# A streaming-encoder trunk on one core: the order of taps and weight splits, one more plain unit, meta values in two passes, the last part by token tile

## The chip, the core and the metric

The kernel runs on one core of one Trainium2 chip. The metric is the device time of one execution in microseconds (us). The engines are named as in the profile: PE is TensorE (matmuls), PEld its weight loads, DVE is VectorE, ACT is ScalarE, POOL is GpSimd, SP is SyncE, which issues most DMAs. Each engine runs its own instructions in the order of the program; where one needs another's result, it waits for a semaphore.

## The reference, cut to what matters

```python
D_MODEL, SEQ, DEPTH, N_META = 1024, 512, 2, 16      # D_FF = 2752, CONV_WIDTH = 31, RET_HEADS = 4
def swiglu_ffn(x, w13, w2):
    a, u = jnp.split(x @ w13, 2, axis=-1)
    return (jax.nn.silu(a) * u) @ w2

def token_mix(h, w_in, ...):
    z = h @ w_in
    xp, ca, cg, q, k, v, g = jnp.split(z, splits, axis=-1)
    y_pool = pool_mixer(xp, pool_w, pool_scale)          # trailing means over 2, 4, 8, 16 tokens
    y_conv = conv_module(ca, cg, ...)                    # u = ca*sigmoid(cg); 31 taps along the tokens; LN; silu; matmul
    y_ret = retention(q, k, v, g, ret_gn_g)              # 4 heads: rotary on q and k, decayed scores, norm, silu(g)
    return jnp.concatenate([y_pool, y_conv, y_ret], axis=-1) @ w_out

def reference(x, meta, ...):
    h = jnp.concatenate([meta, x], axis=1)               # 16 + 512 tokens
    h = layer_norm(h, ln_in_g, ln_in_b)
    for l in range(DEPTH):
        h = layer_norm(ALPHA * h + 0.5 * swiglu_ffn(h, ffn1_w13[l], ffn1_w2[l]), ...)
        h = layer_norm(ALPHA * h + token_mix(h, w_in[l], ...), ...)
        h = layer_norm(ALPHA * h + 0.5 * swiglu_ffn(h, ffn2_w13[l], ffn2_w2[l]), ...)
    return h[:, N_META:]
```

## The kernel before

**Products.** All large products are done in a 32-bit format of PE with the inputs split in a rounded part and a rest (`hi`, `lo`). One product is three matmuls: hi x hi, hi x lo, lo x hi (`mm3`, lines 130 to 135). A weight tile is loaded by SP into a raw buffer, ScalarE casts it to hi, and DVE subtracts to get lo, 512 columns at a time (`weights`, lines 86 to 95). There are five hi and five lo buffers (`WB`), so the split of a weight waits until PE is done with the one five before it.

**Tokens.** Features lie on the partitions. The 528 tokens are two halves, s = 0 and 1, of 256 tokens and 8 meta tokens each: 264 columns. In the last FFN the meta tokens are left out, 256 columns.

**Stages.** They follow each other on PE: f0a, mixer m0, f0b for layer 0, then f1a, m1 and f1b (`last_ffn`) for layer 1. The hidden units of an FFN (22 pieces of 128) are done in five parts (`PARTS`; the first is units 0, 1, 21, 2, 3), and after each part its share of the second product is added to the residual h. The units 0, 1 and 21 of the first part are plain: both halves by both weight columns, 96 matmuls for a unit of two weight tiles. All other units are "summed": from sums of token halves and of weight quarters (`sums`, `sum_weights`), seven products of 12 matmuls take the place of eight. The sums of the tokens are made once in each FFN by DVE, after its norm, and are needed by the first summed unit, which is unit 2.

**Norms.** Between stages stands a layer norm (`normed`, `center`, `inv_var`, `inv_spread`): PE sums over the partitions with a matmul by ones; DVE makes the inverse root in some ten small steps that each wait for the one before (`inv_root`); PE spreads the result again. Half 0 is normed while PE still does half 1's last products. `rooted["first"]` and `rooted["second"]` are the last steps of the two roots. `tc.issue_after(x)` holds the instructions inside it behind x in the order of x's engine.

**Mixer.** First the products for the convolution (`u`) and the pool (`xp`) are made, then the values `v` in five token tiles (four of 128 and the 16 meta tokens, v4), then a loop over the heads with key, query and gate projections (`kp`, `qp`, `gp`, 24 matmuls for a half). Each goes to one of four accumulator banks (`BANKS["acc"]`). DVE turns k and q (`rotary`, the first product reads and so empties the bank), POOL copies the meta columns of k (`km`) for the scores. The convolution's 62 taps (31 for each of two tiles `m0y`) run on DVE, all of them on the same two tiles; the loop takes `PACE[hd]` of them from a generator after each projection:

```python
            for i, _ in enumerate(work(hd, before)):
                for _ in range(PACE[hd]):
                    next(taps, None)
```

**What sets the order.** A scheduler goes through the instructions in program order as a priority and puts on each engine the first one whose inputs and buffers it has. Buffers of a pool (`wide` has 16) are given out in program order. So an instruction far behind in the program can be done early if its engine is free, as the taps are.

**The end.** The last part of the last FFN goes over the two column halves; in the second the token tiles 0 to 3 follow each other, and each is normed and written (`measure`, `root`, `scale`, `leave`).

## Time and profile before

| | |
|---|---|
| median of 3 runs | 1979.4 us (1978.49 to 1981.81) |
| profiled execution | 1979.3 us, span 1977.5 us |
| busy: PE, DVE, ACT, POOL | 1912.4, 1548.9, 920.1, 215.0 us |
| instructions | 36739 |

The span is the time from the first instruction to the last one in the profile; the 1.8 us to the execution's own time lie around it. PE is the engine to look at; DVE, the next, is busy for 78% of the span.

### The profile page before, as it was taken

What the parts mean: (1) busy time and instruction counts of PE and PEld (TensorE: products, weight loads), DVE (VectorE), ACT (ScalarE), POOL (GpSimd) and SP (SyncE); (2) the same over time, 40 slices, a digit from 0 to 9 for tenths busy, and PEclk for the clock granted to TensorE, in tenths of its full rate; (3) what the DMA queues carried; (4) which work ended last, traced back from release to release, by engine and by line L of the source; (5) the groups of instructions that cost most, each with busy time, mean ns of one, the idle gap of its engine ahead of it and who ended that gap; (6) DMA issues with size and microseconds to landing.
All of it is one profiled execution on the core that took longest, in us unless ns stands there. A gap on an engine that the chain in (4) does not pass through costs nothing.

```text
span 1977.5 us, 36739 instructions
## 1 busy us (share of the span) xinstructions
PE 1912.4 (97%) x14423; PEld 1826.3 (92%) x14423; DVE 1548.9 (78%) x3466; ACT 920.1 (47%) x1845; POOL 215.0 (11%) x283
## 2 busy tenths in 40 slices
PE   7999999999999999999999999999999999999996
PEld 6999999997899899999989999998889998999995
DVE  7788778689767977788697787787897697877787
ACT  5454446443333644454464554464343265544451
POOL 4000000442003000000120000005320130000001
PEclk9999999999999999999999999999999999999998
DMA  4422323322112233323213323332131213323321
GB/s 143 129 86 97 116 88 104 100 76 85 63 34 75 64 98 108 97 89 107 95 54 111 101 89 107 97 118 75 65 104 54 65 44 118 107 86 107 107 97 43
DMA packets 61069, 177.98 MB, mean 90 GB/s; under 512 B 6976, under 2 KB 10944, under 8 KB 60896
## 3 DMA queue, kind: packets, MB, share of 16 engines
q1 hardware_dynamic: 59744, 174.59, 27.8%
q8 instruction: 113, 1.85, 0.4%
q10 hardware_dynamic: 1152, 1.05, 0.2%
q14 instruction: 60, 0.49, 0.1%
HBM read 173.52 MB, written 2.10 MB: 89 GB/s over the span
## 4 chain that ended last, share of the span: by engine, by line
PE 79%; DVE 12%; POOL 3%; issue 3%; ACT 2%; DMA 0%; SPq 0%; DVEq 0%; POOLq 0%; ACTq 0%
PE f0a_y L134 2%; PE f0a_y L133 2%; PE f1bo L890 2%; PE f1bo L888 2%; PE f0a_y L135 2%; PE f1bo L889 2%; PE f0b_y L134 2%; PE f1a_y L134 2%; PE f0b_y L133 2%; PE f0b_y L135 2%; PE f1a_y L135 2%; PE f1a_y L133 2%; DVE m0y L610 1%; DVE m1y L610 1%; PE m0sc L719 1%
## 5 line engine op out<-in xcount | busy, mean ns | idle before, releaser
L610 DVE SCALAR_TENSOR_TENSOR m1y<-m1u,vec,m1y 128x528 f32<-128x528 f32 x60 | 46.1, 801 | 0.0
L91 ACT CAST f0a_o_h<-f0a_o_r 128x512 fp32r<-128x512 f32 (+1 forms) x37 | 23.5, 635 | 48.4 <-PE f0a_y L134 29.5
L610 DVE SCALAR_TENSOR_TENSOR m0y<-m0u,vec,m0y 128x528 f32<-128x528 f32 x60 | 45.9, 801 | 0.0
L91 ACT CAST f1a_o_h<-f1a_o_r 128x512 fp32r<-128x512 f32 (+1 forms) x37 | 23.6, 637 | 48.0 <-PE f1a_y L134 29.0
L91 ACT CAST f0b_o_h<-f0b_o_r 128x512 fp32r<-128x512 f32 (+1 forms) x37 | 23.5, 636 | 47.6 <-PE f0b_y L134 29.3
L335 DVE TENSOR_TENSOR x<-x,f0a_y 128x264 f32<-128x264 f32 x64 | 27.1, 425 | 23.3 <-PE f0a_y L135 23.1
L335 DVE TENSOR_TENSOR h<-h,f0b_y 128x264 f32<-128x264 f32 x64 | 27.1, 425 | 23.2 <-PE f0b_y L135 23.1
L335 DVE TENSOR_TENSOR h<-h,f1a_y 128x264 f32<-128x264 f32 x64 | 27.1, 424 | 23.1 <-PE f1a_y L135 23.0
L94 DVE TENSOR_TENSOR f1bw_l<-f1bw_r,f1bw_h 128x512 fp32r<-128x512 f32 x42 | 27.7, 688 | 17.6 <-ACT f1bw_h L91 17.0
L949 POOL TENSOR_TENSOR yt<-yt,g_last 128x256 f32<-128x256 f32 x4 | 3.0, 740 | 337.2 <-ACT yt L948 337.2
L94 DVE TENSOR_TENSOR f0a_o_l<-f0a_o_r,f0a_o_h 128x512 fp32r<-128x512 f32 (+1 forms) x42 | 26.6, 642 | 13.4 <-ACT f0a_o_h L91 11.3
L94 DVE TENSOR_TENSOR f1a_o_l<-f1a_o_r,f1a_o_h 128x512 fp32r<-128x512 f32 (+1 forms) x42 | 26.7, 642 | 13.4 <-ACT f1a_o_h L91 11.4
L94 DVE TENSOR_TENSOR f0b_o_l<-f0b_o_r,f0b_o_h 128x512 fp32r<-128x512 f32 (+1 forms) x42 | 26.7, 642 | 12.6 <-ACT f0b_o_h L91 10.4
L278 POOL TENSOR_TENSOR f0b_ln_s<-h,h 128x264 f32<-128x264 f32 x2 | 1.6, 820 | 313.8 <-DVE h L335 313.8
L587 POOL MEMSET m1u<- 128x30 f32 x2 | 0.2, 123 | 307.6 <-PE f1a_20Q L135 307.6
L587 POOL MEMSET m0u<- 128x30 f32 x2 | 0.2, 123 | 306.1 <-PE f0a_20Q L135 306.1
L91 ACT CAST f1bw_h<-f1bw_r 128x1024 fp32r<-128x1024 f32 (+1 forms) x22 | 22.2, 1011 | 21.0 <-PE f1bo L890 4.2
L894 DVE TENSOR_TENSOR yt<-yt,f1bo 128x256 f32<-128x256 f32 x80 | 27.8, 414 | 5.4 <-PE f1bo L890 5.3
L291 ACT ACTIVATE m_ln_q<-h 128x264 f32<-128x264 f32 (+1 forms) x32 | 11.9, 414 | 39.7 <-DVE h L289 36.1
L257 PE MATMUL tr<-ident,xtok 128*128 128x128 f32 (+1 forms) x48 | 10.9, 328 | 12.1 <-DVE xtok L242 11.4
L281 POOL TENSOR_TENSOR m_ln_s<-m_ln_s,h 128x264 f32<-128x264 f32 (+1 forms) x20 | 18.2, 912 | 32.0 <-DVE h L329 26.1
L257 PEld LDWEIGHTS tr<-ident,xtok 128*128 128x128 f32 (+1 forms) x48 | 6.8, 167 | 16.1 <-issue 14.8
(10805 smaller groups left out, 9335.0 us busy)
## 6 DMA issues: line engine op xcount, KB each, us to landing
f1bw_r<-in_w2last SPq DMA_DIRECT2D x20, 512.0 KB, 3.8
f0a_o_r<-in_w SPq DMA_DIRECT2D x32, 256.0 KB, 2.7
f0b_o_r<-in_w SPq DMA_DIRECT2D x32, 256.0 KB, 2.8
f1a_o_r<-in_w SPq DMA_DIRECT2D x32, 256.0 KB, 2.9
m0wo_r<-in_w_out SPq DMA_DIRECT2D x8, 512.0 KB, 3.5
m1wo_r<-in_w_out SPq DMA_DIRECT2D x8, 512.0 KB, 3.5
m0w_r<-in_w_in SPq DMA_DIRECT2D x6, 512.0 KB, 4.4
m1w_r<-in_w_in SPq DMA_DIRECT2D x6, 512.0 KB, 4.3
```

The costliest lines, as they stand in the source:

```text
L91: nc.scalar.copy(out=hi[:, :n], in_=w[:, :n])
L94: e.tensor_tensor(out=lo[:, sl], in0=w[:, sl], in1=raw(hi[:, sl]), op=ALU.subtract)
L133: nc.tensor.matmul(out, lhsT=wh, rhs=xh, start=start, stop=False, skip_group_check=onto)
L134: nc.tensor.matmul(out, lhsT=wh, rhs=xl, start=False, stop=False, skip_group_check=onto)
L135: nc.tensor.matmul(out, lhsT=wl, rhs=xh, start=False, stop=stop, skip_group_check=onto)
L335: nc.vector.tensor_tensor(out=y, in0=y, in1=ps, op=ALU.add)
L610: nc.vector.scalar_tensor_tensor(out=ys[c], in0=src, scalar=wk, in1=ys[c], op0=ALU.mult, op1=ALU.add)
L719: nc.tensor.matmul(sc[:kn, :cw], lhsT=kk[ks][:, kc : kc + kn], rhs=qq[s][:, c0 : c0 + cw], start=True, stop=True)
L888: nc.tensor.matmul(o, lhsT=hh, rhs=wh, start=part > 0 and i == 0, stop=False)
L889: nc.tensor.matmul(o, lhsT=hh, rhs=wl, start=False, stop=False)
L890: nc.tensor.matmul(o, lhsT=hl, rhs=wh, start=False, stop=i == nk - 1)
L894: nc.vector.tensor_tensor(out=y[:, :256], in0=y[:, :256], in1=o, op=ALU.add)
```

## The change

Six edits are joined.

1. Taps: 28 (`EARLY`) are taken ahead of the loop over the heads; then `PACE` is (1, 1, 2, 2, 0) instead of (4, 3, 3, 2, 0), and each of these taps is held behind the last rotary sum or gate (`made["last"]`). A step of the scores comes ahead of the taps.
2. Splits: the casts and subtractions of the weights of the plain units, and of the mixer's first products, are held behind the norm's first or second root; their DMAs no longer are. `center` puts every other square in another tag's buffers.
3. Unit 2 is plain (`PLAIN = 4`), so unit 3 is the first summed one.
4. v4: hi and lo of the meta tokens lie in one stationary tile of 48 columns (hi, 16 zeros set by POOL, lo). Each weight part then needs one matmul, 16 instead of 24, and a copy and an add join the two results in a new `wide` tile, `vm`.
5. The last part of the last FFN runs over the token tiles, with both column halves of each. Tiles 0 to 2 are normed on ACT, tile 3 on DVE and ACT.
6. At the start the meta rows are scaled on ACT instead of POOL, and first.

```diff
-PACE = (4, 3, 3, 2, 0)
+EARLY, PACE = 28, (1, 1, 2, 2, 0)
@@ weights
-        nc.scalar.copy(out=hi[:, :n], in_=w[:, :n])
-        for c in range(0, n, 512):
-            sl = slice(c, min(c + 512, n))
-            e.tensor_tensor(out=lo[:, sl], in0=w[:, sl], in1=raw(hi[:, sl]), op=ALU.subtract)
+        with hold():
+            nc.scalar.copy(out=hi[:, :n], in_=w[:, :n])
+            for c in range(0, n, 512):
+                sl = slice(c, min(c + 512, n))
+                e.tensor_tensor(out=lo[:, sl], in0=w[:, sl], in1=raw(hi[:, sl]), op=ALU.subtract)
@@ hidden_part
-        plain = PARTS[part][: AHEAD if part == 0 else 0]
+        plain = PARTS[part][: PLAIN if part == 0 else 0]
...
-                late = "first" in rooted and i >= LATE_W
-                with tc.issue_after(rooted["second" if i >= LATE_B else "first"]) if late else nullcontext():
-                    w[u] = unit_weights(u, src, f"{name}_{u}")
+                late = part == 0 and "first" in rooted
+                held["by"] = rooted["second" if i >= LATE_B else "first"] if late else None
+                w[u] = unit_weights(u, src, f"{name}_{u}")
+                held["by"] = None
@@ mixer
+                held["by"] = rooted["first" if kind == "u" else "second"]
                 ws[kind, c] = [weights(w_in[i], 1024, f"{name}w{i}") for i in tiles]
+                held["by"] = None
...
+            pair = sq_pool.tile([P, 48], F32R, tag="xm", name=f"{name}xm{k}", bufs=KT)
+            nc.gpsimd.memset(raw(pair[:, NM:32]), 0.0)
...
+                if tt == 4:
+                    nc.tensor.matmul(ps[:48], lhsT=xm[k], rhs=wh, start=k == 0, stop=False)
+                    nc.tensor.matmul(ps[:48], lhsT=xm[k], rhs=wl, start=False, stop=k == KT - 1)
+                    continue
...
+            if tt == 4:
+                vm = wide(f"{name}vm")
+                nc.scalar.copy(out=vm[:n, :512], in_=ps[32 : 32 + n])
+                nc.vector.tensor_tensor(out=vm[:n, :512], in0=ps[:n], in1=vm[:n, :512], op=ALU.add)
+                ps = vm[:, :512]
...
         taps = conv_taps()
+        for _ in range(EARLY):
+            next(taps)
...
-                for _ in range(PACE[hd]):
-                    next(taps, None)
                 if hd == HEADS or i > 0:
                     next(steps, None)
+                with tc.issue_after(made["last"]):
+                    for _ in range(PACE[hd]):
+                        next(taps, None)
@@ last_ffn
+        for tt in range(4):
+            ts = slice((tt % 2) * P, (tt % 2 + 1) * P)
+            for ch in range(2):
+                for c, cw in ((0, 256), (256, 256)) if (tt, ch) == (3, 1) else ((0, 512),):
+                    o = acc(f"{name}l{tt}{ch}{c}")
+                    for i in range(nk):
...
             measure(tt)
             root(tt)
...
             scale(tt)
-            if tt != 2:
-                leave(tt)
+            leave(tt)
```

How the change moves instructions is seen at three places. First DVE at the first root of the norm between mixer 0 and f0b (`m_ln_v` to `m_ln_dg` are the root's steps, `f0b_..._l` splits of the next FFN's weights, `h` the residual). Before:

```order
1057 L94 TENSOR_TENSOR f0b_0u_l<-f0b_0u_r,f0b_0u_h 128x512
1058 L161 TENSOR_SCALAR m_ln_v<-m_ln_rs 88x3
1059 L94 TENSOR_TENSOR f0b_0u_l<-f0b_0u_r,f0b_0u_h 128x512
1060 L162 TENSOR_SCALAR m_ln_y<-m_ln_v,bits 88x3
1061 L328 SCALAR_TENSOR_TENSOR h_1_7692<-f0a_ln_x4h,m0mo_7667 128x264
1062 L167 SCALAR_TENSOR_TENSOR m_ln_g<-m_ln_y,m_ln_v 88x3
1063 L94 TENSOR_TENSOR f0b_1a_l<-f0b_1a_r,f0b_1a_h 128x512
1064 L169 SCALAR_TENSOR_TENSOR m_ln_w<-m_ln_g,m_ln_y 88x3
1065 L329 SCALAR_TENSOR_TENSOR h_1_7692<-f0a_ln_x4l,h_1_7692 128x264
```

After the change:

```order
1045 L168 TENSOR_SCALAR m_ln_v<-m_ln_rs 88x3
1046 L169 TENSOR_SCALAR m_ln_y<-m_ln_v,bits 88x3
1047 L174 SCALAR_TENSOR_TENSOR m_ln_g<-m_ln_y,m_ln_v 88x3
1048 L176 SCALAR_TENSOR_TENSOR m_ln_w<-m_ln_g,m_ln_y 88x3
1049 L177 SCALAR_TENSOR_TENSOR m_ln_y<-m_ln_w,m_ln_y 88x3
1050 L179 SCALAR_TENSOR_TENSOR m_ln_g<-m_ln_w,m_ln_g 88x3
1051 L333 SCALAR_TENSOR_TENSOR h_1_7683<-f0a_ln_x4h,m0mo_7658 128x264
1052 L176 SCALAR_TENSOR_TENSOR m_ln_w<-m_ln_g,m_ln_y 88x3
1053 L334 SCALAR_TENSOR_TENSOR h_1_7683<-f0a_ln_x4l,h_1_7683 128x264
```

The splits stand behind the root now. Second DVE from the value products to the first rotary product in mixer 0 (`m0y` are the taps, `m0vmu` the means of the value tiles, `m0k00r` the first rotary product). Before:

```order
663 L94 TENSOR_TENSOR m0wv_l<-m0wv_r,m0wv_h 128x512 x5
664 L608 TENSOR_SCALAR m0y_5486<-m0u_5126,vec 128x528
665 L645 TENSOR_TENSOR m0sm_2_5735<-m0sm_2_5735,inv_n 128x16
666 L647 SCALAR_TENSOR_TENSOR m0xp_5259<-m0sm_2_5735,inv_n,m0xp_5259 128x512
667 L646 TENSOR_TENSOR m0xp_5259<-m0sm_2_5735,m0xp_5259 128x16
668 L608 TENSOR_SCALAR m0y_5487<-m0u_5196,vec 128x528
...
679 L610 SCALAR_TENSOR_TENSOR m0y_5487<-m0u_5196,vec,m0y_5487 128x528
680 L684 TENSOR_REDUCE m0vmu_5581<-m0v_5556 128x4
681 L610 SCALAR_TENSOR_TENSOR m0y_5486<-m0u_5126,vec,m0y_5486 128x528
682 L685 TENSOR_SCALAR m0vmu_5581<-m0vmu_5581 128x4
```

After the change:

```order
657 L703 TENSOR_REDUCE m0vmu_5645<-m0v_5620 128x4
658 L704 TENSOR_SCALAR m0vmu_5645<-m0vmu_5645 128x4
659 L703 TENSOR_REDUCE m0vmu_5679<-m0v_5654 128x4
660 L704 TENSOR_SCALAR m0vmu_5679<-m0vmu_5679 128x4
661 L101 TENSOR_TENSOR m0wq_l<-m0wq_r,m0wq_h 128x512 x2
662 L101 TENSOR_TENSOR m0wk_l<-m0wk_r,m0wk_h 128x512 x2
663 L616 TENSOR_SCALAR m0y_5474<-m0u_5114,vec 128x528
664 L700 TENSOR_TENSOR m0vm<-m0v_5688,m0vm 16x512
665 L616 TENSOR_SCALAR m0y_5475<-m0u_5184,vec 128x528
...
693 L618 SCALAR_TENSOR_TENSOR m0y_5475<-m0u_5184,vec,m0y_5475 128x528
...
697 L724 TENSOR_TENSOR m0k00r<-m0kp_0_5769,cosb 128x264
```

The taps began ahead of the first value mean and stand now behind the fourth, behind the splits of wq and wk, and in a block ahead of the rotary product. Third POOL in mixer 0 after the change (`m1xm` are the tiles of mixer 1's meta tokens, `m0sm` the window sums); before, no row stood between the copies for `m0xm` and the window sums:

```order
92 L679 CAST m0xm_5518<-f0a_ln_x7l 128x8
93 L676 MEMSET m1xm_17769 128x16
...
100 L676 MEMSET m1xm_17811 128x16
101 L647 COPY m0sm_1_5751<-m0xp_5247 128x1
102 L650 TENSOR_TENSOR m0sm_1_5751<-m0xp_5247 128x542
103 L647 COPY m0sm_2_5754<-m0sm_1_5751 128x2
104 L650 TENSOR_TENSOR m0sm_2_5754<-m0sm_1_5751 64x541
```

Eight new memsets for the next mixer stand ahead of this mixer's window sums.

## Rows read from the trace of the kernel before

**Rows 1.** The page's busy time of each engine, share of the span, instructions.
```profile
PE 1912.4 (97%) x14423; PEld 1826.3 (92%) x14423; DVE 1548.9 (78%) x3466; ACT 920.1 (47%) x1845; POOL 215.0 (11%) x283
```

**Rows 2.** What PE waited for: us in total, times, longest us.
```profile
PE m0sc L719 <- POOL m0km L794: 3.4, 1, 3.4
PE f1b_2Q L133 <- ACT f1b_2x_hi L415: 3.1, 1, 3.1
PE f0b_2P L135 <- DVE f0b_2a_lo L431: 2.8, 1, 2.8
PE f1a_2P L135 <- DVE f1a_2a_lo L431: 2.5, 1, 2.5
PE f0b_ln_rs L189 <- DVE f0b_ln_q L298: 1.8, 1, 1.8
...
PE f0a_2P L135 <- DVE f0a_2a_lo L431: 1.1, 1, 1.1
```

**Rows 3.** Windows: length, busy us of PE, PEld, DVE, ACT, POOL; PEclk; DMA, GB/s.
```profile
360.00:400.00 40.00, 36.80 (x276) 35.16 (x275) 28.43 (x74) 16.77 (x34) 21.34 (x36) 0.96 0.16 55
455.00:483.00 28.00, 24.62 (x175) 23.31 (x174) 28.00 (x57) 14.01 (x27) 11.68 (x4) 0.88 0.40 128
...
640.00:680.00 40.00, 36.42 (x275) 35.15 (x275) 37.90 (x94) 25.58 (x60) 3.53 (x4) 0.96 0.12 34
...
1020.00:1060.00 40.00, 36.12 (x272) 34.81 (x271) 36.51 (x79) 25.88 (x58) 0.85 (x1) 0.96 0.21 60
...
1630.00:1660.00 30.00, 26.64 (x199) 25.93 (x199) 28.83 (x61) 19.88 (x40) 0.00 (x0) 0.89 0.30 91
```

**Rows 4.** Timeline of PE: start us, us, what [idle before <-releaser].
```profile
449.67 0.40 PE L680 MATMUL m0v<-m0wv_h,m0xm 128*16 128x512 f32 x1
...
455.21 0.28 PE L133 MATMUL m0kp<-f0a_ln_x0h,m0wk_h 128*128 128x264 f32 x1
...
458.12 0.28 PE L133 MATMUL m0kp<-f0a_ln_x0h,m0wk_h 128*128 128x264 f32 x1
...
666.40 0.59 PE L135 MATMUL f0b_2P<-m_ln_x0h,f0b_2a_lo 128*128 128x264 f32 x1 [2.81 <-DVE f0b_2a_lo L431]
```

**Rows 5.** Timeline of DVE in mixer 0: taps, and the first rotary product.
```profile
433.92 5.38 DVE L610 SCALAR_TENSOR_TENSOR m0y<-m0u,vec,m0y 128x528 f32<-128x528 f32 x5
...
446.15 4.15 DVE L610 SCALAR_TENSOR_TENSOR m0y<-m0u,vec,m0y 128x528 f32<-128x528 f32 x6
...
464.52 0.41 DVE L703 TENSOR_TENSOR m0k00r<-m0kp,cosb 128x264 f32<-128x264 f32 x1
```

**Rows 6.** Windows of line 610 alone, the taps.
```profile
430.00:455.00 25.00, 20.65 (x27) 1.00 0.06 22
```

**Rows 7.** Timeline of POOL in mixer 0: window sums, and a copy for the scores.
```profile
423.02 1.26 POOL L642 TENSOR_TENSOR m0sm<-m0xp 128x542 f32<-128x542 f32 x1 [11.98 <-ACT m0xp L597]
...
435.64 1.74 POOL L642 TENSOR_TENSOR m0sm<-m0sm 64x535 f32<-64x535 f32 x1
...
470.14 6.03 POOL L794 COPY m0km<-m0k01r 128x8 f32<-128x8 f32 x1
```

**Rows 8.** Timeline of DVE: the two roots of m_ln ahead of f0b.
```profile
619.88 0.67 DVE L94 TENSOR_TENSOR f0b_0u_l<-f0b_0u_r,f0b_0u_h 128x512 fp32r<-128x512 f32 x1
...
625.20 0.43 DVE L192 SCALAR_TENSOR_TENSOR m_ln_dg<-ident,m_ln_y 88x264 f32<-88x264 f32 x1
...
640.48 0.16 DVE L161 TENSOR_SCALAR m_ln_v<-m_ln_rs 88x3 f32<-88x3 f32 x1
...
642.70 0.43 DVE L192 SCALAR_TENSOR_TENSOR m_ln_dg<-ident,m_ln_y 88x264 f32<-88x264 f32 x1
```

**Rows 9.** Timeline of the end: the last matmul, and the last root's last step.
```profile
1959.53 0.28 PE L889 MATMUL f1bo<-f1bw_l,f1b_20x_h 128*128 128x256 f32 x1
...
1972.26 0.15 DVE L177 TENSOR_SCALAR f1brs_y<-f1brs_y 128x1 f32<-128x1 f32 x1
```

**Rows 10.** Timeline of PE at the start.
```profile
13.14 3.12 PE L257 MATMUL tr<-ident,xtok 8*128 8x8 f32 x11 [0.69 <-POOL xtok L244]
```

More of the change, by code (lines that the diff above doesn't have):

```diff
@@ L83, in col, with hold @@
         return vec[lo:hi, j : j + 1]
+    held = {"by": None}
+    def hold():
+        return tc.issue_after(held["by"]) if held["by"] is not None else nullcontext()
     def weights(src, n, name, e=nc.vector):
@@ L237, in enter @@
         for c in range(2):
-            for i, tt in enumerate(group):
+            for i, tt in reversed(list(enumerate(group))):
                 y = tok[tt][c]
@@ L289, in center @@
             nc.vector.tensor_tensor(out=y[:, :n], in0=y[:, :n], in1=mean[:, :n], op=ALU.subtract)
-            q.append(t(f"{name}_q{i}", "q"))
+            q.append(t(f"{name}_q{i}", "sm" if k > 2 and i % 2 else "q"))
             nc.scalar.activation(q[i][:, :n], y[:, :n], AF.Square)
@@ L697, in mixer @@
             nc.sync.dma_start(out=wpw[k][:, :256], in_=a["pw"][l][:, k * 256 : (k + 1) * 256])
+        made = {}
         def rotary(ps, s, n, nm):
@@ L704, in rotary @@
             nc.vector.tensor_tensor(out=r2[:, :n], in0=r2[:, :n], in1=sinb[:, s, :n], op=ALU.mult)
-            nc.vector.tensor_tensor(out=r[:, :n], in0=r[:, :n], in1=r2[:, :n], op=ALU.add)
+            made["last"] = nc.vector.tensor_tensor(out=r[:, :n], in0=r[:, :n], in1=r2[:, :n], op=ALU.add).ins
             return r
@@ L767, in gate @@
             g = t(f"{name}gs{hd}{s}", "g")
-            nc.scalar.activation(g[:, : no[s]], ps[:, : no[s]], AF.Silu)
+            made["last"] = nc.scalar.activation(g[:, : no[s]], ps[:, : no[s]], AF.Silu).ins
             gg.append(g)
@@ L871, in last_ffn @@
             nk = len(full)
+            if part == len(PARTS) - 1:
+                break
             for ch in range(2):
@@ L896, in last_ffn @@
                 steps = range(-1 if part == 0 else 0, nk)
-                if part == len(PARTS) - 1 and ch == 1:
-                    for tt in range(3):
-                        for i in steps:
-                            step(i, tt)
-                        for j in range(2):
-                            add(tt, j, ps[tt][:, j * 256 : (j + 1) * 256])
-                    for j in range(2):
-                        o = ps[3] if j == 0 else acc(f"{name}o{ch}4")
-                        for i in steps:
-                            step(i, 3, j * 256, 256, o[:, :256])
-                        add(3, j, o[:, :256])
-                else:
-                    for i in steps:
-                        for tt in range(4):
-                            step(i, tt)
-                    for tt in range(4):
-                        for j in range(2):
-                            add(tt, j, ps[tt][:, j * 256 : (j + 1) * 256])
+                for i in steps:
+                    for tt in range(4):
+                        step(i, tt)
+                for tt in range(4):
+                    for j in range(2):
+                        add(tt, j, ps[tt][:, j * 256 : (j + 1) * 256])
             done += nk
@@ L935, in scale @@
             for j, y in enumerate(yt[tt]):
[L936 removed]
+                if tt < 3:
                     break
@@ L956, in leave @@
                 (nc.sync if j % 2 else nc.scalar).dma_start(out=a["out"][tt * P : (tt + 1) * P, j * 256 : (j + 1) * 256], in_=y)
-        for tt in range(4):
+        c0 = done * 512
+        w_last = [[], []]
+        for i in range(0, nk, 2):
+            cw = min(2, nk - i) * 512
+            for ch, make in enumerate((weights, weights_wide)):
+                w = make(a["w2last"][ch, :, c0 + i * 512 : c0 + i * 512 + cw], cw, f"{name}l{ch}{i}")
+                w_last[ch] += w if ch else [at(w, slice(c, c + 512)) for c in range(0, cw, 512)]
+        for tt in range(4):
+            ts = slice((tt % 2) * P, (tt % 2 + 1) * P)
[3 more added lines that the diff above has]
+                    for i in range(nk):
+                        wh, wl = (x[:, c : c + cw] for x in w_last[ch][i])
+                        hh, hl = at(hid[full[i]][tt // 2], ts)
+                        nc.tensor.matmul(o[:, :cw], lhsT=hh, rhs=wh, start=i == 0, stop=False)
+                        nc.tensor.matmul(o[:, :cw], lhsT=hh, rhs=wl, start=False, stop=False)
+                        nc.tensor.matmul(o[:, :cw], lhsT=hl, rhs=wh, start=False, stop=i == nk - 1)
+                    for k in range(0, cw, 256):
+                        y = yt[tt][2 * ch + (c + k) // 256]
+                        nc.vector.tensor_tensor(out=y[:, :256], in0=y[:, :256], in1=o[:, k : k + 256], op=ALU.add)
             measure(tt)
             root(tt)
-            if tt == 3:
-                with tc.issue_after(met[tt]):
-                    leave(2)
             scale(tt)
-            if tt != 2:
-                leave(tt)
+            leave(tt)
     load_tokens((4, 0, 1))
```

27 lines of the change are left out of this document (12 added, 15 removed).

## The prediction

> **What bounds the kernel now.** The page's first part says it: TensorE (PE) is busy for 97% of the span [rows 1], and nearly all of that is matmuls that must be done. So a change gains only where PE stands idle, runs at the lower of its clock levels, or gets fewer matmuls; it loses where one of the three grows. I therefore read next the list of what PE waited for [rows 2]. It names short waits of a few kinds: at the start of each summed unit 2 (f0a_2, f0b_2, f1a_2, f1b_2, on a split made by VectorE or ScalarE), at each norm (a sum of squares or a root made by VectorE, DVE below), and in each mixer at the first scores (on GpSimd's copy m0km, 3.4 us). The windows of these places [rows 3] show idle time and clock together: in 455 to 483 PE is busy for 24.6 of 28 us at a mean clock of 0.88, in 640 to 680 for 36.4 of 40 at 0.96. The clock has two levels, 1.2 and 2.4 GHz, and a row shows the lower one behind a wait: after 2.81 us of waiting, the matmul at 666.40 takes 0.59 us [rows 4].
>
> Prices of a matmul are start to start [rows 4]: the 24 matmuls of the fifth value tile take from 449.67 to 455.21, 0.231 us each at 512 columns; the 24 of a projection take from 455.21 to 458.12, 0.121 us each at 264.
>
> **Plain unit 2, in four FFNs.** A plain unit has 2 products x 8 x 3 x 2 halves = 96 matmuls, a summed one 7 x 4 x 3 = 84. That adds 12 x 4 = 48 matmuls at 0.121 us, **5.8 us** lost. In return the first summed unit comes 96 matmuls (11.6 us) later, and DVE has to do only four splits more ahead of it (0.67 us for one in [rows 8]), 2.6 us. PE waited there 3.1, 2.8, 2.5 and 1.1 us [rows 2], far below the 9 us won, so these 9.5 us should go. With them go the slow stretches: 40 x 0.04 = 1.6 us in 640 to 680, 1.6 in 1020 to 1060, 30 x 0.11 = 3.3 in 1630 to 1660 [rows 3], 6.5 in all. Bounds: all 16 us go (gain 10.2), or the wait only moves to unit 3 (loss 5.8). In the new order of DVE the splits of unit 2 stand among the token sums and those of unit 3 right behind them, some 5 us ahead of the new need by these prices, so I take a **gain of 10**.
>
> **Splits behind the root.** In the first root of m_ln DVE comes from a split inside it at 619.88 to the end of its last step at 625.63, with more splits and residual adds in between; the second root, with almost nothing in between, takes from 640.48 to 643.13 [rows 8]. So a root gets some 3 us shorter. But PE has out-projection or FFN products to do while a first root runs, and the splits held back (0a and 0u, or the first mixer weights) now stand behind the root and ahead of the first product. What PE really loses at a norm is small: 1.8 us for the sum of squares in each FFN norm [rows 2], 3.2 us idle and 1.6 us of clock around the norm ahead of mixer 0 [rows 3]. Gain at least nothing (the splits are now what is late), at most some 2 to 3 us at each of five norms, 12 in all. I take **4.5**, nearer to nothing, because the held splits eat most of the root's gain.
>
> **Mixers: v4.** The fifth value tile needs 16 matmuls of 512 columns instead of 24: 8 x 0.231 = 1.85 us less in each mixer. It is part of the sum that follows.
>
> **Mixers: where the taps now stand.** This is the part that speaks against the change. Before, DVE does 27 of the 62 taps between 430 and 455 [rows 6], while PE does the value matmuls and asks nothing else of DVE. In the changed order (second piece of the order above) no tap stands there. The first tap stands behind the means of value tiles 0 to 3 and behind the splits of wq0 and wk1, and these need buffers that only v4's own first matmuls set free. The 28 EARLY taps then stand in one block, and ahead of the first rotary product (`m0k00r`), which is what empties the bank of `m0kp00`. PE has four banks for accumulators: after kp00, kp01, qp00 and qp01 the next projection, kp10, needs kp00's.
>
> On the times of before: v4 begins at 449.67, and its 16 matmuls end at 453.4. The first buffer comes free at about 450.6; a cast (1 us, put in by me) and four splits of 0.65 us bring the block's begin to about 454.2. A tap costs 0.69 us (six in 4.15) or 1.08 us while GpSimd works on the pool windows (five in 5.38) [rows 5]. In mixer 0 GpSimd's window sums also come late: eight memsets for mixer 1's `xm` stand ahead of them and wait for v4's matmuls (third piece of the order). They took from 423.0 to 437.4, some 12 us of it work [rows 7], so about 11 taps run at 1.08 and 17 at 0.69: 23.6 us. I put 1.5 us for the meta tile's add and mean and 1 for three window operations; then the rotary product begins at about 480.3 instead of 464.52 [rows 5], and kp10 at 480.6. PE's four projections end at 453.4 + 4 x 2.91 = 465.0. So PE stands for about **15 us** where nothing waited before.
>
> Not all of this is lost. Before, kp11 ended at about 472.7 and PE then waited until 476.2 for m0km (3.4 us, [rows 2]); after the new wait, kp10 and kp11 take 5.8 us and, as I put it, 1.7 more at the low clock, to 488, and m0km has been made meanwhile. The scores begin 12 us later. The slow stretch that before followed (28 x 0.12 = 3.4 us, [rows 3]) is then over, so 8.5 us stay. Behind that, 27 taps instead of 15 are left for the later heads, 12 x 0.69 = 8 us on a DVE with little room; I put 1.5 us for it. Mixer 0: **10 us lost**. In mixer 1 no memsets stand ahead of the window sums, all 28 taps run at 0.69 (19.3 us), and the loss is some 4 us smaller: **6.5**. Together **16.5**, v4's gain included. Bounds: nothing lost but v4's gain kept (+3.7), if the wait is hidden by something that I don't see; or 28 taps at 1.08 (30 us) in both mixers, 17 lost in mixer 0 and 15 in mixer 1.
>
> These two tap prices are rows and need no rule. The Trainium skill, "SBUF — State Buffer", section "Who interferes with whom", says that a DVE instruction with two SBUF inputs and a GpSimd one that reads SBUF exclude each other for a whole instruction; the trace agrees with it in both directions (1.08 against 0.69 us for a tap here, and a copy of 128x8 that took 6.03 us beside a dense DVE [rows 7]). By that rule the block and the window sums stretch each other, which is the slow rival below.
>
> **Start.** ScalarE takes the meta rows from GpSimd, for which PE waited 0.69 us [rows 10]: gain **0.7**, bounds 0 and 2.
>
> **End by token tile.** The last matmul begins at 1959.53 and the span ends at 1977.5 [rows 9]: nearly 18 us in which the tiles 1 to 3 are finished one between the other; the last root ends at 1972.4, 5.1 us before the end. Now only tile 3's second half follows the last matmul: an add and a statistic (0.8), aggregate (0.3), a dense root (2.65, as [rows 8]), the same 5.1, about 0.8 for one more GpSimd add, and 1 to 2 us of tile 2 still in DVE's queue: 11 us. Gain **6.5**, bounds 4 (tile 2 in the way) and 8. Its weights must all be split when the part begins; unit 20's own products run meanwhile, and I cost that at nothing; if they came late, 1 to 2 us.
>
> **Sum.** 0.7 + 10 + 4.5 + 6.5 - 16.5 = 5.2 us gained. The profiled execution took 1979.3 us (span 1977.5 and 1.8 around it), 0.1 below the median of 1979.4. Forecast: **1974 us**.
>
> **The rivals.**
> A, the block is hidden: PE finds work or the wait at kp10 is short. For it: DVE is idle in the value stage, so anything let through there shortens the block. Against it: the order on DVE is fixed, and kp10's bank has one releaser. Time: 1979.3 - 21.7 - 3.7 = 1954.
> B, on the other side, slower: the block runs at the slow price. If all 28 taps cost 1.08 us the mixers lose 17 + 15 = 32 and the time is 1979.3 - 21.7 + 32 = 1990; it decides once the mixers lose more than the 21.7 us of gains, 11 each, which in mixer 0 is a mean tap of 0.9 us. For it: the 1.08 of [rows 5]; against it: GpSimd has 12 us of work there, not 30.
> C, the stalls move and don't vanish: the wait of unit 2 turns up at unit 3 for half of its length, the held splits are late by what the root gains. The FFNs give 2 instead of 10, the norms 0: 1979.3 - 0.7 - 2 - 6.5 + 16.5 = 1987.
> D, gains and losses cancel: within 4 us of before, for instance norms at 0 and units at 8.
>
> **How the numbers follow.** The forecast with its own range, 1967 to 1981, has 0.50 (of which 0.35 below 1975.4, 0.11 within 0.2% and 0.04 above); A 0.20; B 0.15; C 0.06; D 0.09. A measurement of this kernel can tell about 0.2%, 4 us. Faster: 0.35 + 0.20 = 0.55. Same: 0.11 + 0.09 = 0.20. Slower: 0.04 + 0.15 + 0.06 = 0.25. The range leaves out the far end of A and of B: 1956 to 1990.
>
> **What would show it.** Right: no tap of m0y before the end of the value matmuls; PE idle 10 to 15 us ahead of kp10 in both mixers, released by DVE's m0k00r, with a slow clock behind it; no wait at f0b_2 or f0b_3; the last matmul about 11 us before the end. Wrong: taps at 430 to 455, or waits on unit 3's splits, or a last part that waits for its weights. The forecast fails most easily on the length of the wait at kp10.

## The result and the profile after

The changed kernel takes **2001.2 us** (median of 4 runs, 2000.0 to 2002.7) against 1979.0 beside it: a ratio of 1.011 [1.010, 1.012], slower by 22 us, outside the range of the forecast. Its profiled execution has a span of 1998.2 us, 20.7 more than before. The page's first part, to lay beside [rows 1]:

```profile
span 1998.2 us, 36754 instructions
PE 1913.1 (96%) x14455; PEld 1831.4 (92%) x14455; DVE 1529.3 (77%) x3431; ACT 915.3 (46%) x1832; POOL 196.6 (10%) x294
```

What PE waited for, the list that answers to [rows 2]:

```profile
PE m0kp L140 <- DVE m0k00r L724: 13.5, 1, 13.5
...
PE m1kp L140 <- DVE m1k00r L724: 10.9, 1, 10.9
PE f0a_0p L141 <- POOL x_l L273: 2.9, 2, 2.2
PE m1pu L141 <- DVE f1a_ln_x6l L325: 2.9, 1, 2.9
PE m0pu L141 <- DVE f0a_ln_x6l L325: 2.9, 1, 2.9
PE m0gp L142 <- DVE m0wg_l L101: 2.6, 1, 2.6
PE f1a_0p L141 <- DVE f0b_ln_x4l L323: 2.5, 2, 2.2
```

The waits of the units (f0a_2 to f1b_2) and the two on m0km and m1km are gone, as forecast (at unit 3, now the first summed one, 0.3 to 0.9 us are left in each FFN), and the wait at kp10 stands where it was forecast: 13.5 us in mixer 0, 10.9 in mixer 1. Four kinds of 2.5 us and more were not forecast: on `x6l` ahead of each mixer, on `x4l` in f1a, on `m0wg_l`, and on `x_l` at the start. The windows (busy us of each engine, then PE's mean clock) answer to [rows 3]:

```profile
400.00:455.00 55.00, 55.00 (x356) 49.45 (x355) 22.81 (x57) 18.85 (x45) 6.09 (x24) 1.00 0.28 92
455.00:500.00 45.00, 28.48 (x180) 26.02 (x178) 38.93 (x70) 13.13 (x28) 30.97 (x20) 0.77 0.10 33
640.00:680.00 40.00, 36.94 (x289) 35.51 (x289) 38.77 (x93) 24.70 (x60) 12.10 (x14) 1.00 0.23 67
1360.00:1410.00 50.00, 44.89 (x321) 42.94 (x321) 36.95 (x97) 23.51 (x51) 23.75 (x54) 0.90 0.16 54
```

DVE is busy for only 22.81 of the 55 us that hold the rest of the first products and most of the value stage (its matmuls begin at 430.30), and in the 45 us behind it PE for 28.48, at a mean clock of 0.77. The first product of mixer 1 lies in the fourth window: there too PE stands idle and then runs slower.

**The balance by stages.** For each stage I read the start of its first matmul on PE's timeline in both traces and took after minus before; the difference from one such landmark to the next is what that stretch lost (+) or gained (-):

| stretch | measured, us | forecast, us |
|---|---|---|
| start and the first units of the four FFNs (to unit 4's first matmul): +1.4 -2.2 -0.2 -3.6 | -4.6 | -10.7 |
| rest of f0a, f0b, f1a with its norm (to the next stage's first matmul): -2.4 -1.7 -2.1 | -6.2 | -4.5 for norms |
| first stage of the mixers (m0pu to m0v, m1pu to m1v): +4.0 +6.4 | +10.4 | in the row above |
| rest of the mixers (m0v to f0b_0p, m1v to f1b_0p): +15.6 +8.3 | +23.9 | +16.5 |
| rest of f1b | -0.2 | 0 |
| after the last matmul | -2.6 | -6.5 |
| sum | +20.7 | -5.2 |

The start and the units came out 6.1 us worse than forecast, the norms with the first stage of the mixers 8.7, the rest of the mixers 7.4, and the end 3.9. Of the mixers' 23.9 us, 5.5 (2.8 and 2.7) are lost from the first matmul of the output projection on.

### The profile page after: what moved, and what is told of

Same layout as the page of the kernel before. It is cut to its first block, busy times and chain, and to the rows that moved or that the text cites. A ratio compares the mean times of both kernels' runs of the same rounds, so it can differ in the third digit from the quotient of the medians.

```text
span 1998.2 us, 36754 instructions
## 1 busy us (share of the span) xinstructions
PE 1913.1 (96%) x14455; PEld 1831.4 (92%) x14455; DVE 1529.3 (77%) x3431; ACT 915.3 (46%) x1832; POOL 196.6 (10%) x294
## 4 chain that ended last, share of the span: by engine, by line
PE 79%; DVE 11%; ACT 2%; POOL 2%; issue 2%; DMA 0%; POOLq 0%; ACTq 0%; DVEq 0%; SPq 0%
PE f1a_y L141 2%; PE f0a_y L141 2%; PE f0b_y L141 2%; PE f1a_y L142 2%; PE f0b_y L142 2%; PE f0a_y L142 2%; PE f0b_y L140 2%; PE f1a_y L140 2%; PE f0a_y L140 2%; PE f1bo L916 1%; PE f1bo L914 1%; PE f1bo L915 1%; POOL m0sm L650 1%; DVE m1y L618 1%; PE m0o L759 1%
## 5 line engine op out<-in xcount | busy, mean ns | idle before, releaser
L101 DVE TENSOR_TENSOR f0b_o_l<-f0b_o_r,f0b_o_h 128x512 fp32r<-128x512 f32 (+1 forms) x42 | 26.6, 642 | 13.5 <-ACT f0b_o_h L98 11.4
L101 DVE TENSOR_TENSOR f1bw_l<-f1bw_r,f1bw_h 128x512 fp32r<-128x512 f32 x32 | 20.9, 688 | 9.5 <-ACT f1bw_h L98 9.1
L650 POOL TENSOR_TENSOR m0sm<-m0sm 64x541 f32<-64x541 f32 (+3 forms) x4 | 23.7, 5926 | 0.2
L98 ACT CAST f1bw_h<-f1bw_r 128x1024 fp32r<-128x1024 f32 x16 | 16.7, 1050 | 12.3 <-PE f1b_10Q L141 1.8
L920 DVE TENSOR_TENSOR yt<-yt,f1bo 128x256 f32<-128x256 f32 x64 | 21.9, 415 | 0.0
L262 PEld LDWEIGHTS tr<-ident,xtok 128*128 128x128 f32 (+1 forms) x48 | 6.9, 166 | 15.6 <-issue 15.0
```

The lines of the kernel that those rows point to most:

```text
L98: nc.scalar.copy(out=hi[:, :n], in_=w[:, :n])
L101: e.tensor_tensor(out=lo[:, sl], in0=w[:, sl], in1=raw(hi[:, sl]), op=ALU.subtract)
L650: nc.gpsimd.tensor_tensor(out=dst[b:, w_:], in0=cur[b:, w_:], in1=cur[b:, : W - w_], op=ALU.add)
L920: nc.vector.tensor_tensor(out=y[:, :256], in0=y[:, :256], in1=o, op=ALU.add)
```

## The experiments

Each ran on the chip beside the kernel before, whose medians there were 1979.5 to 1980.5 us. "After" is the changed kernel.

### 1. Is the block of taps late because of the taps' edit, or of the value tile's buffer?

The forecast read the block ahead of kp10 off the new order and counted it as the price of the taps' own edit. The rival was `vm`, the buffer of the new value tile: it is taken from the ring of 16 wide buffers (line 127), from which the taps' `m0y` and the window sums `m0sm` also come, and it is asked for ahead of them. If the ring hands out its buffers in the order in which they are asked for, then `vm`, which is needed only behind the last value matmuls, holds back in the order of issue all that is asked for behind it. GpSimd's window sums, which began at 423.02 [rows 7], begin at 456.69 in after, and `vm` is first written at 457.55. **vm_own** gives it a buffer of another ring:

```diff
-                vm = wide(f"{name}vm")
+                vm = wp.tile([P, 1024], F32, tag="raw", name=f"{name}vm", bufs=RAW)
```

> The changed kernel, with one line changed: the tile that joins the two results of the meta values (vm) comes from the pool of raw weights, not from the 'wide' pool, in which the tiles of the taps lie. Theory S (the slot): vm is given out ahead of the taps' tiles in the wide pool, so no tap can begin before the fifth value tile; with vm elsewhere the taps are back in the value stage, PE's waits of 13.5 and 10.9 us ahead of kp10 go, and the time falls from 2001 by 14 to 20 us, to 1981 to 1987. Rival E (the 28 early taps, or the hold behind the last rotary sum, make the block by themselves): both waits stay at over 8 us and the time stays within 5 us of 2001.

Measured: 1984.6 us, ratio 1.0024 [1.0013, 1.0036]; 16.6 us of the loss are gone, and the waits on m0k00r and m1k00r with them. In their place, from the list of PE's waits:

```profile
PE m1kp L140 <- ACT m1wk_h L98: 4.6, 1, 4.6
PE m0kp L140 <- ACT m0wk_h L98: 4.6, 1, 4.6
```

`vm` now holds one of the buffers that the weights of the keys need; a new wait, but a smaller one. **taps_old** does the opposite: `vm` as in after, the taps' edit undone.

```diff
-EARLY, PACE = 28, (1, 1, 2, 2, 0)
+EARLY, PACE = 0, (4, 3, 3, 2, 0)
...
-                with tc.issue_after(made["last"]):
-                    for _ in range(PACE[hd]):
-                        next(taps, None)
+                for _ in range(PACE[hd]):
+                    next(taps, None)
```

> The changed kernel with its first edit undone: no early taps, PACE (4, 3, 3, 2, 0), taps not held, as before; vm stays in the wide pool. Theory S: the first tap still stands behind the fourth value mean, but the taps come four to a projection and not in a block of 28; the waits ahead of kp10 shrink to a few us, DVE then has the taps to do among the heads and the time is 1990 to 2000. Rival E: the taps are back in the value stage and the time is 1979 to 1986.

Measured: 2001.7 us, 1.011 [1.009, 1.013]: no gain at all, and outside both expectations. The block ahead of kp10 is gone, but the wait only sits elsewhere, at the scores, where three or four taps now stand ahead of each step:

```profile
PE m0sc L740 <- DVE m0sm L751: 12.6, 3, 10.1
PE m1sc L740 <- DVE m1sm L751: 12.4, 3, 8.4
```

**before_v4_only** puts the value tile's edit, with `vm` wide, alone into the kernel before:

```diff
-            pair = sq_pool.tile([P, 2, NM], F32R, tag="xm", name=f"{name}xm{k}", bufs=KT)
+            pair = sq_pool.tile([P, 48], F32R, tag="xm", name=f"{name}xm{k}", bufs=KT)
...
+            if tt == 4:
+                vm = wide(f"{name}vm")
...
```

> The kernel before with the fourth edit alone: meta values in two passes, vm in the wide pool. Theory S: the taps stand behind the value stage by this edit alone; 12 to 22 us slower than before, though PE has 3.7 us less to do. Rival (the slot matters only with the early taps in a block): 2 to 4 us faster than before, or no change.

Measured: 1998.3 us, 1.009 [1.006, 1.012]. One of the six changes makes 18 us of loss by itself, with the same wait at the scores:

```profile
PE m0sc L739 <- DVE m0sm L750: 12.6, 3, 10.0
```

So the loss does not need the taps' edit. That the buffer makes it, and not the rest of the value tile's edit, is what vm_own and the next run show.

**vm_in_h** has `vm` in two half tiles of a ring that is free there, and the held splits undone (experiment 2), so that neither is left:

```diff
-                vm = wide(f"{name}vm")
+                vm = [t(f"{name}vm{q}", "h")[:, :256] for q in range(2)]
...
```

> vm_own_free_splits, but vm lies in two half tiles of the residual's pool (tag h, which the mixer leaves free) and not in the pool of raw weights. Theory W (vm in the raw pool held up the load of wk0): the 4.6 us that PE waited for m0wk_h and m1wk_h go, and it is 9 to 14 us faster than vm_own_free_splits, 1956 to 1962. Rival: those waits come back under another name and the time stays at 1967 to 1972.

Measured: 1956.0 us, 0.988 [0.985, 0.990], faster than before by 24.5. It differs from held_free_only (experiment 2, 1990.3 us) in the place of `vm` alone, so the wide buffer costs 34.3 us there. VectorE's timeline from ahead of the value stage on, in this kernel:

```profile
418.74 0.55 DVE L613 TENSOR_SCALAR m0y<-m0u,vec 128x528 f32<-128x528 f32 x1
...
426.44 1.32 DVE L613 TENSOR_SCALAR m0y<-m0u,vec 128x528 f32<-128x528 f32 x1
427.68 13.32 DVE L615 SCALAR_TENSOR_TENSOR m0y<-m0u,vec,m0y 128x528 f32<-128x528 f32 x13
...
460.06 0.41 DVE L724 TENSOR_TENSOR m0k00r<-m0kp,cosb 128x264 f32<-128x264 f32 x1
```

and in after:

```profile
457.82 1.32 DVE L616 TENSOR_SCALAR m0y<-m0u,vec 128x528 f32<-128x528 f32 x1
...
461.47 17.05 DVE L618 SCALAR_TENSOR_TENSOR m0y<-m0u,vec,m0y 128x528 f32<-128x528 f32 x25
479.51 0.17 DVE L653 TENSOR_TENSOR m0sm<-m0sm,inv_n 128x16 f32<-128x16 f32 x1 [0.98 <-POOL m0sm L650]
...
481.25 0.42 DVE L724 TENSOR_TENSOR m0k00r<-m0kp,cosb 128x264 f32<-128x264 f32 x1
```

With the same edit of the taps the first one starts 39 us earlier, and the block of 28 ends at 449.90, ahead of PE's first projection (455.85); 13 of them take 1.02 us each while GpSimd makes its window sums, and PE does not wait for it. The first rotary product comes 21 us earlier. GpSimd's eight memsets, which the forecast had in the way of the window sums, stand behind them here. How the ring holds the rest back is not shown: no trace names a buffer, and a ring of 17 was not run.

In after the matmul of kp10 that waited starts at the lower of the two clock levels (granted clock 0.50 from 481.70 to 485.00; 0.42 us for a matmul where 0.28 is usual):

```profile
481.72 0.59 PE L140 MATMUL m0kp<-f0a_ln_x0h,m0wk_h 128*128 128x264 f32 x1 [13.54 <-DVE m0k00r L724]
482.11 0.42 PE L141 MATMUL m0kp<-f0a_ln_x0l,m0wk_h 128*128 128x264 f32 x1
```

### 2. What do the held splits cost?

**vm_own_free_splits** is vm_own with the splits of the plain units and of the mixers' first weights issued as before; **held_free_only** is after (with `vm` wide) with the same edit:

```diff
-                late = part == 0 and "first" in rooted
-                held["by"] = rooted["second" if i >= LATE_B else "first"] if late else None
-                w[u] = unit_weights(u, src, f"{name}_{u}")
-                held["by"] = None
+                late = "first" in rooted and i >= 2
+                with tc.issue_after(rooted["second" if i >= LATE_B else "first"]) if late else nullcontext():
+                    w[u] = unit_weights(u, src, f"{name}_{u}")
...
-                held["by"] = rooted["first" if kind == "u" else "second"]
...
```

> vm_own, and the second edit undone: the casts and subtractions of the weights of the plain units and of the mixers' first products are held behind a root only where they were before. Theory H (the held splits come too late): the waits of the mixers' first products on f0a_ln_x6l and f1a_ln_x6l (2.9 us each) and of f1a_0p (2.5 us) go or shrink, and it is 5 to 12 us faster than vm_own. Rival R (the shorter roots pay for the splits): it is 3 to 8 us slower than vm_own, with waits at the norms' roots.

> The changed kernel (1998.2 us of span, 2001.2 median) with one edit undone: the splits of the first units and of the mixers' first weights are issued as before, not behind the norm's root. The value tile's buffer stays the wide one. If the held splits and the late value buffer cost independently of each other, the kernel loses the 14.3 us that the same edit gave beside the other buffer: about 1987 us, with PE's waits on x4l and x6l gone and those on m0kp and m1kp (13.5 and 10.9 us) still there. If they overlap (a later u stage hands the mixers work that would otherwise stand at kp), less is given back: 1992 to 2000 us and a longer wait at kp.

Measured: 1970.3 us, 0.995 [0.993, 0.997], and 1990.3 us, 1.005 [1.003, 1.007]. Holding the splits back costs 14.3 us beside the one buffer (more than the 5 to 12 expected) and 10.9 beside the other, where the two losses overlap in part. The forecast had a gain of 4.5. Both places take part, as the fastest kernel (experiment 3, 1951.5 us) shows with one of them held at a time, **held_units_alone** (the first of the two edits above left as in after) and **held_mixers_alone** (the second):

```diff
 held_units_alone
-                held["by"] = rooted["first" if kind == "u" else "second"]
 held_mixers_alone
-                held["by"] = rooted["second" if i >= LATE_B else "first"] if late else None
```

> The fastest kernel so far (1951.5 us, no held splits beyond those of before) with the splits of the FFNs' plain units held behind the norm's root, the mixers' weights free. Theory: the units have four products' weights in line and PE misses them only at x4l in the second layer (2.5 us), while the mixers' u stage misses them most; so this costs little: 1952 to 1956 us. Rival: the units are the cost (their first stretch gave 6 us less than the same edit without holding): 1960 to 1966 us.

> The fastest kernel so far (1951.5 us) with only the mixers' first input weights held behind the norm's root, the units' free. Theory: this is where the loss is: the first weights' third and fourth split come only behind the second half's subtractions, PE waits for x6l (2.9 us) in both mixers and runs at the low clock behind it: 1959 to 1964 us. Rival: 1951 to 1954 us, the units being the cost.

Measured: 1959.0 us, 0.988 [0.986, 0.991], and 1958.0 us, 0.988 [0.986, 0.990]: 7.6 and 6.6 us, together about the 14.3. My guess that the units cost little was wrong. PE's waits in the first:

```profile
PE f1a_0p L141 <- DVE f0b_ln_x4l L325: 2.6, 2, 2.3
PE m_ln_mean L290 <- DVE m_ln_s L288: 1.5, 2, 1.2
...
PE f1a_0p L140 <- ACT f0b_ln_x3h L319: 1.2, 1, 1.2
```

and in the second:

```profile
PE m1pu L141 <- DVE f1a_ln_x6l L327: 2.9, 1, 2.9
PE m0pu L141 <- DVE f0a_ln_x6l L327: 2.9, 1, 2.9
```

Of the units' loss 3.9 us lie between the first matmul of f1a and its first output product, where the first and the last wait of that list stand; the rest is not traced to one place. How the mixers' loss comes about shows in after on VectorE, at the norm of f0a (a row with x8 is eight instructions in line), and on PE:

```profile
382.40 1.28 DVE L101 TENSOR_TENSOR m0w_l<-m0w_r,m0w_h 128x512 fp32r<-128x512 f32 x2
...
391.23 2.79 DVE L294 TENSOR_TENSOR x<-x,f0a_ln_mean 128x264 f32<-128x264 f32 x8
...
394.35 0.97 DVE L325 SCALAR_TENSOR_TENSOR f0a_ln_x6l<-x,vec,f0a_ln_x6h 128x264 fp32r<-128x264 f32 x1
...
396.13 0.68 DVE L101 TENSOR_TENSOR m0w_l<-m0w_r,m0w_h 128x512 fp32r<-128x512 f32 x1
```

```profile
395.37 0.47 PE L141 MATMUL m0pu<-f0a_ln_x6l,m0w_h 128*128 128x264 f32 x1 [2.92 <-DVE f0a_ln_x6l L325]
395.64 0.42 PE L142 MATMUL m0pu<-f0a_ln_x6h,m0w_l 128*128 128x264 f32 x1
```

On VectorE in before, at the same norm:

```profile
385.27 0.68 DVE L94 TENSOR_TENSOR m0w_l<-m0w_r,m0w_h 128x512 fp32r<-128x512 f32 x1
...
392.20 2.80 DVE L289 TENSOR_TENSOR x<-x,f0a_ln_mean 128x264 f32<-128x264 f32 x8 [0.48 <-PE f0a_ln_mean L283]
...
396.16 0.48 DVE L320 SCALAR_TENSOR_TENSOR f0a_ln_x4l<-x,vec,f0a_ln_x4h 128x264 fp32r<-128x264 f32 x1
```

The eight subtractions of the second half come ahead of the last normalized rows of the first half in both kernels; before, `x6l` is made only at 398.56. What has changed are the splits of the weights. Before, eight of them were done inside the root, the last by 385.95, and PE had the products of the other weight tiles to do while the rows came. In after two follow the root (382.40), and the next stands at 396.13, behind the subtractions. So PE has nothing left after its matmul at 392.16, waits for `x6l`, and goes on at 0.42 us a matmul.

### 3. The start, the fourth unit, and the end

**vm_in_h_old_start** is vm_in_h with the meta rows on GpSimd again:

```diff
-            for i, tt in reversed(list(enumerate(group))):
+            for i, tt in enumerate(group):
...
+                elif i == 2:
+                    nc.gpsimd.tensor_scalar(out=y, in0=y, scalar1=mv[:p, i, 0:1], scalar2=rs[:p, i : i + 1], op0=ALU.subtract, op1=ALU.mult)
```

> vm_in_h, and the sixth edit undone: the meta rows on GpSimd at the start. Theory: the start's order is not what keeps f0a back (its first part ends 1.4 us late in the changed kernel); within 1.5 us of vm_in_h. Rival: the edit makes GpSimd late with x_l (waits of 0.8 and 2.2 us), and undoing it is 2 to 4 us faster.

Measured: **1951.5 us**, 0.985 [0.983, 0.987], the fastest kernel of the study, 4.5 us below vm_in_h: the run's rival was right, its theory not. ScalarE's timeline in after:

```profile
10.88 2.93 ACT L251 ACTIVATE xtok<-xtok,in_nb,in_y 8x512 f32<-8x512 f32 x4 [0.64 <-DVE in_nb L243]
...
19.06 1.03 ACT L98 CAST f0a_0u_h<-f0a_0u_r 128x1024 fp32r<-128x1024 f32 x1
```

and in vm_in_h_old_start:

```profile
10.93 1.52 ACT L253 ACTIVATE xtok<-xtok,in_nb,in_y 128x512 f32<-128x512 f32 x2 [0.25 <-DVE in_nb L243]
12.35 1.03 ACT L98 CAST f0a_0u_h<-f0a_0u_r 128x1024 fp32r<-128x1024 f32 x1
```

Two more activations (1.4 us) make the cast of the first unit's weights lose its place in ScalarE's line: it comes 6.7 us later, behind the transposed rows (in vm_in_h too, at 19.77). GpSimd's first split of these weights comes late with it (20.89 in vm_in_h, 15.30 without the edit), its `x_l` stands behind that split, and PE waits for `x_l`.

**vm_in_h_plain3** is vm_in_h with three plain units (the last number back from 4 to 3):

```diff
-SKEW, SKEW_F, AHEAD, PLAIN = 6, 8, 3, 4
+SKEW, SKEW_F, AHEAD, PLAIN = 6, 8, 3, 3
```

> vm_in_h, and the third edit undone: unit 2 is summed again. Theory U (the plain unit pays once the splits are free): three FFNs lose 3 to 4.5 us each by undoing it, f0a wins some, and it is 6 to 12 us slower than vm_in_h. Rival (the plain unit costs its 5.8 us of matmuls and wins nothing): it is 4 to 6 us faster.

Measured: 1969.2 us, 0.995 [0.994, 0.996]: the plain unit is worth 13.3 us where nothing else is late, more than the run expected and more than the forecast's upper bound of 10.2. The waits of [rows 2] are back, to the tenth:

```profile
PE f1b_2Q L140 <- ACT f1b_2x_hi L420: 3.1, 1, 3.1
PE f0b_2P L142 <- DVE f0b_2a_lo L436: 2.8, 1, 2.8
...
PE f1a_2P L142 <- DVE f1a_2a_lo L436: 2.5, 1, 2.5
```

**vm_own_old_end** is vm_own with the last FFN's output in before's order (both column halves by unit, tile 2 left behind tile 3's statistics):

```diff
-            if part == len(PARTS) - 1:
-                break
...
```

> vm_own, and the fifth edit undone: the last part of the last FFN as before, over the column halves. Theory Q (the new order of the end leaves tile 2 in DVE's queue and wins little): 2 to 3 us slower than vm_own, with 17 to 18 us behind the last matmul instead of 15.3. Rival (the prediction's 6.5 us): 5 to 8 us slower than vm_own.

Measured: 1987.5 us, 1.0037 [1.0026, 1.0049], 3 us more than vm_own: the new end gains some 3 (1 to 5 by the spread of the ten runs of each), not 6.5. In the two profiles 15.3 and 17.9 us follow the start of the last matmul. VectorE's timeline in after says why:

```profile
1987.30 0.76 DVE L963 TENSOR_TENSOR yt<-yt,g_last 128x256 f32<-128x256 f32 x2
1987.97 0.76 DVE L964 TENSOR_TENSOR yt<-yt,b_last 128x256 f32<-128x256 f32 x2
...
1988.97 0.42 DVE L216 BATCH_NORM_STATS2 f1b_st<-yt 128x6 f32<-128x256 f32 x1
```

Tile 2's products and sums stand ahead of tile 3's last statistic, which comes 6 us after the last matmul's start (1982.9), where the forecast's terms put it at 2 to 3. **leave2_on_gpsimd** moves them off VectorE, in the fastest kernel:

```diff
-                    e = nc.gpsimd if tt < 2 else nc.vector
-                    e.tensor_tensor(out=y, in0=y, in1=g_[j][:, :256], op=ALU.mult)
-                    nc.vector.tensor_tensor(out=y, in0=y, in1=b_[j][:, :256], op=ALU.add)
+                    nc.gpsimd.tensor_tensor(out=y, in0=y, in1=g_[j][:, :256], op=ALU.mult)
+                    (nc.gpsimd if tt == 2 else nc.vector).tensor_tensor(out=y, in0=y, in1=b_[j][:, :256], op=ALU.add)
```

> The fastest kernel so far (1951.5 us: value buffer in half tiles, splits as before, meta rows as before) with tile 2's eight products and sums at the end moved from VectorE to GpSimd. Theory: they stand in VectorE's queue ahead of tile 3's last statistics, 8 x 0.34 = 2.7 us of it; so the end after the last matmul gets 2 to 3 us shorter: about 1949 us. Rival: GpSimd takes 8 x 0.78 = 6.2 us for them and is then in the way of tile 3's own two sums, or slows VectorE beside it: 1951 to 1954 us.

Measured: 1952.3 us, 0.986 [0.985, 0.987]: no gain. The queue was as I thought, since tile 3's root now begins 3.8 us after the last matmul's start (1938.40 against 1934.60) instead of 7.0. But what was won there was lost in the root, as VectorE's rows show:

```profile
1938.40 0.15 DVE L168 TENSOR_SCALAR f1brs_v<-f1bmv 128x1 f32<-128x1 f32 x1
...
1940.78 0.67 DVE L176 SCALAR_TENSOR_TENSOR f1brs_w<-f1brs_g,f1brs_y 128x1 f32<-128x1 f32 x1
```

GpSimd beside it, and the same step of the root in the fastest kernel:

```profile
1940.52 0.91 POOL L965 TENSOR_TENSOR yt<-yt,b_last 128x256 f32<-128x256 f32 x1
```

```profile
1942.85 0.15 DVE L176 SCALAR_TENSOR_TENSOR f1brs_w<-f1brs_g,f1brs_y 128x1 f32<-128x1 f32 x1
```

A step on one column takes 0.67 us instead of 0.15 while GpSimd works beside it on two tensors, and ends as that work ends (1941.45 and 1941.43). The root ends 6.6 us after it began (1945.04), against 3.2 in the fastest kernel.

### 4. What the other edits are worth where nothing else is late

In the fastest kernel (1951.5 us) one more edit was undone at a time. **taps_old_vm_free** has the edit of taps_old; **v4_old_vm_free** the 24 matmuls of the fifth value tile again; **squares_old_buffer** the squares of the norms in one ring of buffers:

```diff
 v4_old_vm_free
+                xh, xl = xm[k] if tt == 4 else at(xs[k][tt // 2], slice(tt % 2 * P, (tt % 2 + 1) * P))
...
-                if tt == 4:
...
-                    nc.tensor.matmul(ps[:48], lhsT=xm[k], rhs=wh, start=k == 0, stop=False)
...
 squares_old_buffer
-            q.append(t(f"{name}_q{i}", "sm" if k > 2 and i % 2 else "q"))
+            q.append(t(f"{name}_q{i}", "q"))
```

> The fastest kernel so far (1951.5 us) with the taps' edit undone: no early block, three or four taps in front of each step. Theory: with the value buffer out of the way the new order of taps costs nothing and even saves the waits of before on m0km and m1km (3.4 and 3.5 us) with the slow clock behind them (about 3 us each): undone, 1951.5 + 7 to 14 = 1958 to 1965 us. Rival, the model of the forecast: the block of 28 taps ahead of the first rotary product costs mixer time by itself; undone, the kernel gets faster, 1940 to 1950 us.

> The fastest kernel so far (1951.5 us) with the fifth value tile computed as before: 24 matmuls instead of 16 and no vm buffer, eight more rows of copies for it. Theory: the two passes are worth their 8 x 0.231 us in each mixer once the buffer is free: 1951.5 + 3.7 = 1955 us. Rival: copy, add and four more dependent steps of the meta tile take back what the matmuls give: 1950 to 1952.5 us.

> The fastest kernel so far (1951.5 us) with the norms' squares in one buffer tag as before, no alternation. PE's waits on the sum of squares in the FFN norms were 1.8 us before and are 1.0 now; if the alternation does that, three FFN norms get 0.8 us each back and the time is about 1954 us; if the order of the splits does it, nothing changes: 1951.5 us.

Measured: 1957.5 us, 0.989 [0.987, 0.990]; 1953.6 us, 0.987 [0.985, 0.988]; 1955.4 us, 0.987 [0.985, 0.988]. So with its buffers free the taps' edit gains 6.1 us (a little under my bounds), the two-pass value tile 2.2 (between theory and rival), and the squares' second ring 4.0: without it PE waits again for the sums, as in [rows 2]:

```profile
PE f0a_ln_rs L196 <- DVE f0a_ln_q L305: 1.9, 1, 1.9
```

The edits now add up. Undone one by one from the best kernels they cost 6.1 (taps), 13.3 (unit, from vm_in_h), 2.2 (value tile), 4.0 (squares) and 3.0 (end, from vm_own): from 1951.5 that leads to 1980.1, where before took 1979 to 1980.5. Each of the five is known to 1 or 2 us, and two of them from another kernel, so a match this close is in part luck. In the other direction the start (4.5), the wide buffer (1990.3 - 1956.0 = 34.3, with the splits free) and the held splits (10.9) lead from 1951.5 back to 2001.2; these are steps of one path from kernel to kernel, so their sum is no test of its own.

## Why the prediction was wrong

By the steps of experiment 4 the splits came out 15.4 us worse than forecast, the mixers 9.5 (26.0 lost: 34.3 to the buffer, less 6.1 and 2.2 gained), the start 5.2 and the end 3.5. The units gave 3.3 more than forecast, and the squares' ring 4.0.

- **Splits behind the root: the term that failed.** "Gain at least nothing" was no bound, and 4.5 was 11 to 14 us lost (experiment 2). The root did get dense and the norms did get shorter (-6.2 in the balance, a part of it by the squares' ring). But I only set the held splits against the root, and not against what comes behind it on the same engine: the normalized rows of the first half and the second half's eight subtractions, which now go ahead of all but the first splits. PE, which before had the products of these weights to fill the time until the last rows came, waits for those rows and then runs slowly. The sentence "the splits are now what is late" named it without a price. It should have had one: in f0a the second tile's split came 13.7 us behind the first's (396.13 against 382.40), which left PE 2.9 us without work, with the slow clock of [rows 4] behind the wait.
- **Mixers: right in the wait, too small in the whole, wrong in cause.** Forecast 16.5, measured 23.9 by the stages. The wait at kp10 was right (13.5 us for 15), as was its place: the rotary product was forecast for 480.3 and came at 481.25, and mixer 0's scores came 11.7 us later within the mixer where the forecast had 12. What failed behind it are two terms. The forecast took 3.4 us of slow clock off as "then over", but a wait of 2.6 us on `m0wg_l` follows (mean clock 0.72 from 492 to 498), and 12.8 us are lost up to the output projection instead of 8.5. And the output projection lost 2.8 and 2.7 instead of 1.5 each. As to the cause, the order that I read (no tap in the value stage) was not the taps' edit: it was `vm` in the ring of wide buffers (experiment 1). Against rival A the forecast held that the order on VectorE is fixed; with `vm` elsewhere the same block is done before the projections begin and costs nothing. The output projection's 2.8 and 2.7 are the taps left for later: the fastest kernel loses 2.7 and 4.1 there too, and with the taps' edit undone in it (taps_old_vm_free) that stretch loses nothing.
- **Units: right, under-sized, and masked.** 10 forecast, 13.3 measured on its own, above the forecast's best case of 10.2: the forecast left out six shorter waits at unit 2, of 0.2 to 0.8 us, which make 3.0 us in PE's list of before; in after the held splits took back a part of it, so the units with the start show 4.6.
- **Start: wrong sign.** +0.7 became -4.5. I priced the wait that goes and not the cast that loses its turn on ScalarE.
- **End: right mechanism, half of the size.** 6.5 forecast, some 3 measured; the failing number is "1 to 2 us of tile 2 still in DVE's queue": tile 3's root begins 7.0 us after the start of the last matmul, not 2 to 3.
- **Value tile.** 3.7 forecast for its matmuls, 2.2 measured; the sum of 16.5 took it in.
- **Squares' ring.** It was in the diff and had no term of its own, that is, it was put at nothing; it is worth 4.0 us.

No rival was this case: B (slow block, 1990) has the right side, but the taps did not slow down (25 took 17.05 us, 0.68 each). C named the held splits as late, but only by what the roots gain, and left the mixers at 16.5.
